# Last stage of a hybrid DeltaNet / HGRN2 block: gates stored in row order, the final norm on three engines, stores from GpSimd's queue, a third bank for the branch products

## The chip, the cores and the metric

One core of a Trainium2 chip. The metric is the device time of one execution in microseconds (us). All arithmetic is float32; products on TensorE split each float32 into a high and a low part of type fp32r and sum three passes (high x high, low x high, high x low).

## The reference, cut to what matters

A block over 2048 latent tokens (a grid of 32 rows and 64 columns, in row order) with a prefix of 256 context tokens. Two token mixers (A: gated DeltaNet, in row order; B: HGRN2, in column order) give `o_a` and `o_b`; then

```
def merge_branches(o_a, o_b, p, ...):
    y_a = rms_norm_gated(o_a, a_norm_l, p['a_gate']) @ w_a_out_l      # o * rsqrt(mean o^2) * gain * silu(gate)
    y_b = rms_norm_gated(o_b, b_norm_l, p['b_gate']) @ w_b_out_l
    gates = sigmoid(p['merge'])                                       # 2 x 1024 per token
    return (gates[0] * y_a + gates[1] * y_b) @ w_out_l
...
h_lat = layer_norm(alpha * h_lat + gate_l * sub_lat) * ln_g + ln_b
```

`a_gate`, `b_gate` and `merge` are columns of one input projection `u @ w_in`: 8 blocks of 128 columns for the branch gates, 16 for the merge gates.

## The kernel before, in words

The stages up to about 1862 us are the normalised and modulated input, the input projection (24 matmuls of 512 columns for each block of 128 outputs and 512 tokens), the convolution, and the two scans. Latent tokens are kept there in column order. `gate_block` (L212) makes one gate block: it projects, evicts the PSUM tile into `gt` (ScalarE on odd token groups L218, VectorE on even L220) and stores it in DRAM as `gT`; 24 blocks x 4 groups = 96 evictions, spread over the whole program.

The last stage (L1136 on) goes over 8 tiles of 256 tokens (4 grid columns x 32 rows, twice), `tg` = 0..7. For each tile:

- `pre(tg)`: loads the two mixers' outputs (`o`), takes 16 sums of squares on ScalarE (L1046), a power on GpSimd (L1050), scales (L1052). For four pairs of heads it loads the gate (`gt`), forms the gated SiLU (L1063, L1064), transposes `o` on TensorE into PSUM `ptw` (L1069), multiplies (L1071), and splits into `yh` (ScalarE, L1072) and `yl` (GpSimd, L1073). `o` is in row order within 128 tokens and the gate in column order, so L1071 reads PSUM through `by_row`.
- `branch_y(tg)`: for `m` = 0..7 (blocks of 128 of the 1024 channels) loads the two merge gates (`mg`, three buffers, L1082), takes their sigmoid (ScalarE, L1083), makes 24 matmuls of 256 columns into one PSUM bank `py` (L1089 to L1091; two banks, pool `pj2`, in turn), multiplies by the gates (VectorE, L1092), adds the branches (L1093), and splits into `mh` (ScalarE, L1095) and `ml` (VectorE, L1096). The last two write with `by_row`, 16 bytes apart, to turn column order into row order.
- `emit(tg)`: for two halves `t` of 128 tokens loads `x` into `xt` (two buffers), makes 2 x 24 matmuls of 512 columns (`pso`, L1109 to L1111), adds (L1112), takes the statistics (L1117 to L1119 and the power on GpSimd, L1120), normalises: VectorE (x - mean) * rs (L1130), GpSimd times `lng` (L1131), GpSimd plus `lnb` (L1132), and SyncE's queue stores it (L1133). The last tile has its own tail (L1121 to L1128), which the change doesn't touch.

All loads and stores stand in one queue, SyncE's (SP), in program order; a waiting entry holds what is behind it. A scheduler sets each engine's order of instructions from its own model of time, so the tiles overlap: `pre(tg + 1)` runs within tile `tg`, and the first three `mg` loads of a tile are made during the tile before. PSUM in the last stage: `py` 2 banks, `ptw` 3, `pso` 3.

Of the kernel before, what the change touches and what calls it, by code (L numbers as in the profile page):

```python
# [8 lines left out]
F32 = mybir.dt.float32  # L9
F32R = mybir.dt.float32r  # L10
U8 = mybir.dt.uint8
AF = mybir.ActivationFunctionType
ALU = mybir.AluOpType
# [3 lines left out]
P = 128  # L17
# [6 lines left out]
GR = SEQ // GW  # L24
# [15 lines left out]
def block_kernel(ctx, tc, x, c, ctx_in, c_ctx, w_mod, b_mod, w_in, conv_w, a_log, dt_bias,  # L40
                 lb_param, a_norm_g, b_norm_g, w_a_out, w_b_out, w_out, ln_g, ln_b, out, dbg=None):
    nc = tc.nc
    sy, te, ve, ac, po = nc.sync, nc.tensor, nc.vector, nc.scalar, nc.gpsimd
# [17 lines left out]
    MLV = 1  # L61
# [100 lines left out]
    def by_row(ap):  # L162
        return ap.rearrange("p (t r c) -> p t c r", r=GR, c=4)

    def by_col(ap):
        return ap.rearrange("p (t c r) -> p t c r", r=GR, c=4)

# [44 lines left out]
    def gate_block(i, groups, psum=None, tag="pj", w=None):  # L212
        w = w or load_w(gcol[i])
        for g in groups:
            ps = proj(w, g, psum or pg_[0], tag)
            t = re.tile([P, GT], F32, tag="acc", name="gt", bufs=2)
            if g % 2:
                ac.copy(out=t, in_=ps)  # L218
            else:
                ve.tensor_copy(out=t, in_=ps)  # L220
            sy.dma_start(out=gT[i, :, g * GT:g * GT + GT], in_=t)


# [788 lines left out]
    with tc.tile_pool(name="ww", reuse_waits="tile", bufs=2) as ww, \  # L1012
# [22 lines left out]
        def pre(tg):  # L1035
# [21 lines left out]
            for k in range(0, 8, 2):  # L1057
                i, h = divmod(k, H)
                gt = (wpp.tile([P, 2, TG], F32, tag="ws", name="gt", bufs=1) if tg == 0 and k == 6 else
                      ww.tile([P, 2, TG], F32, tag="g", name="gt", bufs=GBF))  # L1060
                sy.dma_start(out=gt, in_=gT[k:k + 2, :, tg * TG:tg * TG + TG].rearrange("h p t -> p h t"))
                sg = ww.tile([P, 2, TG], F32, tag="sg", name="sgt", bufs=SGB)
                ac.activation(out=sg, in_=gt, func=AF.Sigmoid)  # L1063
                ve.scalar_tensor_tensor(out=gt, in0=gt, scalar=cols[:, R_GA + i:R_GA + i + 1], in1=sg,  # L1064
                                        op0=ALU.mult, op1=ALU.mult)
                pt = pw_.tile([P, 2, TG], F32, tag="t", name="ptw", bufs=3)
                for j in range(2):
                    for t in range(2):
                        te.transpose(pt[:, j, t * P:t * P + P], on[t][:, i, h + j, :], ident)  # L1069
                gf = by_col(gt.rearrange("p j t -> p (j t)"))  # L1070
                last[0] = ve.tensor_tensor(out=gf, in0=by_row(pt.rearrange("p j t -> p (j t)")), in1=gf, op=ALU.mult).ins  # L1071
                ac.copy(out=yh[i][:, h:h + 2, :], in_=gt)  # L1072
                po.tensor_tensor(out=yl[i][:, h:h + 2, :], in0=gt, in1=yh[i][:, h:h + 2, :].bitcast(F32), op=ALU.subtract)  # L1073
            return yh, yl

        def branch_y(tg, yh, yl):
            mh = ww.tile([P, KB, TG], F32R, tag="mh", name="mh", bufs=1)
            ml = ww.tile([P, KB, TG], F32R, tag="ml", name="ml", bufs=1)
            for m in range(KB):
                mg = (wpp.tile([P, 2, TG], F32, tag="ws", name="mg", bufs=1) if MG3 and m % 3 == 2 else  # L1080
                      re.tile([P, 2, TG], F32, tag="acc", name="mg", bufs=2))
                sy.dma_start(out=mg, in_=gT[8 + m:24:8, :, tg * TG:tg * TG + TG].rearrange("i p t -> p i t"))  # L1082
                ac.activation(out=mg, in_=mg, func=AF.Sigmoid)  # L1083
                py = pj[0].tile([P, 2, TG], F32, tag="pj", name="py")
                ms_ = slice(m * P, m * P + P)
                for i in range(2):
                    wh, wl = wab[i]
                    for k in range(H):
                        te.matmul(out=py[:, i, :], lhsT=wh[:, k, ms_], rhs=yh[i][:, k, :], start=(k == 0), stop=False)  # L1089
                        te.matmul(out=py[:, i, :], lhsT=wh[:, k, ms_], rhs=yl[i][:, k, :], start=False, stop=False)  # L1090
                        te.matmul(out=py[:, i, :], lhsT=wl[:, k, ms_], rhs=yh[i][:, k, :], start=False, stop=(k == H - 1))  # L1091
                ve.tensor_tensor(out=mg, in0=py, in1=mg, op=ALU.mult)  # L1092
                ve.tensor_tensor(out=mg[:, 0], in0=mg[:, 0], in1=mg[:, 1], op=ALU.add)  # L1093
                mm, hm, lm = by_col(mg[:, 0]), by_row(mh[:, m, :]), by_row(ml[:, m, :])
                ac.copy(out=hm, in_=mm)  # L1095
                (ve if MLV else po).tensor_tensor(out=lm, in0=mm, in1=hm.bitcast(F32), op=ALU.subtract)  # L1096
            return mh, ml

        def emit(tg, mh, ml):
            for t in range(2):  # L1100
# [26 lines left out]
                                                op0=ALU.mult, op1=ALU.add)  # L1127
                        sy.dma_start(out=out_cm[:, 4 * cc:4 * cc + 4, ns], in_=xt[:, ns])  # L1128
                else:
                    ve.tensor_scalar(out=xt, in0=xt, scalar1=mv[:, 0:1], scalar2=rs_, op0=ALU.subtract, op1=ALU.mult)  # L1130
                    po.tensor_tensor(out=xt, in0=xt, in1=lng, op=ALU.mult)  # L1131
                    po.tensor_tensor(out=xt, in0=xt, in1=lnb, op=ALU.add)  # L1132
                    sy.dma_start(out=out_cm[:, 4 * cc:4 * cc + 4], in_=xt)  # L1133


        while late[0] < NLATE:  # L1136
# [52 lines left out]
```

## Time and profile before

| | us |
|---|---|
| median of 3 runs (lowest, highest) | 2328.68 (2319.0, 2331.19) |
| the profiled execution | 2322.79 |
| its span in the trace | 2321.1 |
| TensorE busy, share of the span | 2210.0, 95% |
| VectorE, ScalarE, GpSimd busy | 1401.9, 907.8, 756.9 |
| last matmul of the program starts | 2312.21 |

The profiled execution is 1.7 us longer than its span. TensorE is busy nearly throughout. A matmul's listed duration overlaps the next one's, so the time that it takes is read from the distance of two starts.

### The profile page before, as it was taken

What the parts mean: (1) busy time and instruction counts of PE and PEld (TensorE: products, weight loads), DVE (VectorE), ACT (ScalarE), POOL (GpSimd) and SP (SyncE); (2) the same over time, 40 slices, a digit from 0 to 9 for tenths busy, and PEclk for the clock granted to TensorE, in tenths of its full rate; (3) what the DMA queues carried; (4) which work ended last, traced back from release to release, by engine and by line L of the source; (5) the groups of instructions that cost most, each with busy time, mean ns of one, the idle gap of its engine ahead of it and who ended that gap; (6) DMA issues with size and microseconds to landing.
All of it is one profiled execution on the core that took longest, in us unless ns stands there. A gap on an engine that the chain in (4) does not pass through costs nothing. (4 is left out here: it accounts for less than half of the span.)

```text
span 2321.1 us, 39923 instructions
## 1 busy us (share of the span) xinstructions
PE 2210.0 (95%) x14998; PEld 1848.3 (80%) x14998; DVE 1401.9 (60%) x3184; ACT 907.8 (39%) x2298; POOL 756.9 (33%) x736
## 2 busy tenths in 40 slices
PE   7899999999999999999989999999989889999998
PEld 2778888888888888888878778788878878878887
DVE  5926666636766667774374877872332358566655
ACT  3523222234343444432434445544544454344321
POOL 3613343302221122224534445311133234334341
PEclk8999999999999999999999999999999999999999
DMA  8312222322322322224656588786887855434322
GB/s 317 112 36 73 66 73 71 87 63 78 92 71 85 91 74 87 85 76 132 178 163 195 185 243 256 206 240 204 250 271 264 264 192 166 127 110 128 118 82 78
DMA packets 298329, 330.24 MB, mean 142 GB/s; under 512 B 77536, under 2 KB 216918, under 8 KB 298136
## 3 DMA queue, kind: packets, MB, share of 16 engines
q1 hardware_dynamic: 298135, 327.69, 45.9%
q8 instruction: 118, 1.93, 0.4%
q14 instruction: 76, 0.61, 0.1%
HBM read 216.83 MB, written 110.79 MB: 141 GB/s over the span
## 5 line engine op out<-in xcount | busy, mean ns | idle before, releaser
L205 PE MATMUL ps<-uhi,wh 128*128 128x512 f32 (+1 forms) x1824 | 707.9, 388 | 5.4 <-DVE uhi L293 2.6
L206 PE MATMUL ps<-ulo,wh 128*128 128x512 f32 (+1 forms) x1824 | 705.8, 387 | 3.0 <-DVE ulo L295 2.7
L207 PE MATMUL ps<-uhi,wl 128*128 128x512 f32 (+1 forms) x1824 | 706.2, 387 | 0.5 <-POOL wl L197 0.5
L205 PEld LDWEIGHTS ps<-uhi,wh 128*128 128x128 f32 x1824 | 345.6, 190 | 71.0 <-DVE uhi L293 3.9
L206 PEld LDWEIGHTS ps<-ulo,wh 128*128 128x128 f32 x1824 | 345.7, 190 | 66.8 <-DVE ulo L295 3.9
L207 PEld LDWEIGHTS ps<-uhi,wl 128*128 128x128 f32 x1824 | 345.2, 189 | 64.5 <-POOL wl L197 1.3
L197 POOL TENSOR_TENSOR wl<-ws,wh 128x512 fp32r<-128x512 f32 x144 | 192.2, 1335 | 536.7 <-ACT wh L196 512.3
L196 ACT CAST wh<-ws 128x512 fp32r<-128x512 f32 x144 | 89.5, 621 | 288.5 <-DMA ws<-in_w_in_dram 192.3
L1089 PE MATMUL py<-yh,wab 128*128 128x256 f32 x512 | 151.4, 296 | 26.5 <-DVE mg L1092 25.6
L393 DVE SCALAR_TENSOR_TENSOR acc<-raw,cols,acc 128x512 f32<-128x512 f32 x192 | 153.9, 855 | 0.8
L1090 PE MATMUL py<-yl,wab 128*128 128x256 f32 x512 | 148.3, 290 | 2.6 <-POOL yl L1073 2.6
L1091 PE MATMUL py<-yh,wab 128*128 128x256 f32 x512 | 147.9, 289 | 0.0
L1089 PEld LDWEIGHTS py<-yh,wab 128*128 128x128 f32 x512 | 100.7, 197 | 31.0 <-DVE mg L1092 29.0
L572 POOL TENSOR_TENSOR bg<-s,fz 128x512 f32<-128x512 f32 (+1 forms) x36 | 38.0, 1057 | 263.5 <-ACT X L552 96.9
L1109 PE MATMUL pso<-uhi,mh 128*128 128x512 f32 x256 | 102.9, 404 | 3.6 <-ACT mh L1095 2.3
L1090 PEld LDWEIGHTS py<-yl,wab 128*128 128x128 f32 x512 | 101.0, 197 | 3.8 <-POOL yl L1073 3.2
L1111 PE MATMUL pso<-uhi,ml 128*128 128x512 f32 x256 | 102.0, 404 | 2.0 <-DVE ml L1096 1.9
L1110 PE MATMUL pso<-ulo,mh 128*128 128x512 f32 x256 | 101.6, 399 | 0.0
L1091 PEld LDWEIGHTS py<-yh,wab 128*128 128x128 f32 x512 | 101.2, 198 | 0.0
L1073 POOL TENSOR_TENSOR yl<-gt,yh 128x512 fp32r<-128x512 f32 x32 | 46.7, 1478 | 165.2 <-ACT yh L1072 165.2
L1096 DVE TENSOR_TENSOR ml<-mg,mh 128x256 fp32r<-128x256 f32 x64 | 53.0, 832 | 70.1 <-ACT mh L1095 69.4
L1095 ACT CAST mh<-mg 128x256 fp32r<-128x256 f32 x64 | 41.2, 651 | 135.7 <-DVE mg L1093 135.4
(371 smaller groups left out, 4135.8 us busy)
## 6 DMA issues: line engine op xcount, KB each, us to landing
ws<-in_w_in_dram SPq DMA_DIRECT2D x144, 256.0 KB, 3.2
gT<-gt SPq DMA_DIRECT2D x96, 256.0 KB, 3.2
kv<-knvD SPq DMA_DIRECT2D x36, 512.0 KB, 5.4
kq<-qkvD SPq DMA_DIRECT2D x32, 512.0 KB, 5.5
an<-atN SPq DMA_DIRECT2D x32, 512.0 KB, 5.7
mg<-gT SPq DMA_DIRECT2D x64, 256.0 KB, 3.6
qkvD<-acc SPq DMA_DIRECT2D x48, 256.0 KB, 2.3
l<-qkvD SPq DMA_DIRECT2D x16, 768.0 KB, 5.1
```

The costliest lines, as they stand in the source:

```text
L196: ac.copy(out=wh[:, j:j + 4, :], in_=ws)
L197: po.tensor_tensor(out=wl[:, j:j + 4, :], in0=ws, in1=wh[:, j:j + 4, :].bitcast(F32), op=ALU.subtract)
L205: te.matmul(out=ps, lhsT=wh[:, k, :], rhs=uhi[gi][:, k, :], start=(k == 0), stop=False)
L206: te.matmul(out=ps, lhsT=wh[:, k, :], rhs=ulo[gi][:, k, :], start=False, stop=False)
L207: te.matmul(out=ps, lhsT=wl[:, k, :], rhs=uhi[gi][:, k, :], start=False, stop=(k == KB - 1))
L393: ve.scalar_tensor_tensor(out=a_, in0=raw[:, o + k:o + k + n], scalar=wk, in1=a_, op0=ALU.mult, op1=ALU.add)
L1089: te.matmul(out=py[:, i, :], lhsT=wh[:, k, ms_], rhs=yh[i][:, k, :], start=(k == 0), stop=False)
L1090: te.matmul(out=py[:, i, :], lhsT=wh[:, k, ms_], rhs=yl[i][:, k, :], start=False, stop=False)
L1091: te.matmul(out=py[:, i, :], lhsT=wl[:, k, ms_], rhs=yh[i][:, k, :], start=False, stop=(k == H - 1))
L1109: te.matmul(out=ps, lhsT=mh[:, k, ts_], rhs=wout[0][k][:, ns], start=(k == 0), stop=False)
L1110: te.matmul(out=ps, lhsT=mh[:, k, ts_], rhs=wout[1][k][:, ns], start=False, stop=False)
L1111: te.matmul(out=ps, lhsT=ml[:, k, ts_], rhs=wout[0][k][:, ns], start=False, stop=(k == KB - 1))
```

## The change

It touches four things.

1. `gate_block` turns the order at eviction: the output is written through `as_rows` (contiguous) and the PSUM tile is read through `col_to_row` (steps of 32 elements), so `gT` holds row order. L1071, `mh` and `ml` then need no rearrangement and read and write contiguously.
2. `py` of m = 2 and 5 goes to a bank of its own (tag `y` of pool `pw`); `ptw` has 2 banks instead of 3.
3. The final norm of tiles 0 to 6: a small VectorE operation forms -mean * rs (`nm`), ScalarE applies scale and bias, VectorE multiplies by `lng`, GpSimd adds `lnb`.
4. The store of tiles 0 to 6 is issued by GpSimd (`po.dma_start`) instead of SyncE.

```diff
+    def col_to_row(ap):
+        return ap.rearrange("p (t c r) -> p t r c", r=GR, c=4)
+    def as_rows(ap):
+        return ap.rearrange("p (t r c) -> p t r c", r=GR, c=4)
...
             if g % 2:
-                ac.copy(out=t, in_=ps)
+                ac.copy(out=as_rows(t), in_=col_to_row(ps))
             else:
-                ve.tensor_copy(out=t, in_=ps)
+                ve.tensor_copy(out=as_rows(t), in_=col_to_row(ps))
...
-                pt = pw_.tile([P, 2, TG], F32, tag="t", name="ptw", bufs=3)
+                pt = pw_.tile([P, 2, TG], F32, tag="t", name="ptw", bufs=2)
...
-                gf = by_col(gt.rearrange("p j t -> p (j t)"))
-                last[0] = ve.tensor_tensor(out=gf, in0=by_row(pt.rearrange("p j t -> p (j t)")), in1=gf, op=ALU.mult).ins
+                last[0] = ve.tensor_tensor(out=gt, in0=pt, in1=gt, op=ALU.mult).ins
...
-                py = pj[0].tile([P, 2, TG], F32, tag="pj", name="py")
+                py = (pw_.tile([P, 2, TG], F32, tag="y", name="py", bufs=1) if m % 3 == 2 else
+                      pj[0].tile([P, 2, TG], F32, tag="pj", name="py"))
...
-                mm, hm, lm = by_col(mg[:, 0]), by_row(mh[:, m, :]), by_row(ml[:, m, :])
-                ac.copy(out=hm, in_=mm)
-                (ve if MLV else po).tensor_tensor(out=lm, in0=mm, in1=hm.bitcast(F32), op=ALU.subtract)
+                ac.copy(out=mh[:, m, :], in_=mg[:, 0])
+                (ve if MLV else po).tensor_tensor(out=ml[:, m, :], in0=mg[:, 0], in1=mh[:, m, :].bitcast(F32), op=ALU.subtract)
...
-                    ve.tensor_scalar(out=xt, in0=xt, scalar1=mv[:, 0:1], scalar2=rs_, op0=ALU.subtract, op1=ALU.mult)
-                    po.tensor_tensor(out=xt, in0=xt, in1=lng, op=ALU.mult)
+                    nm_ = ww.tile([P, 1], F32, tag="nm", name="nm2")
+                    ve.scalar_tensor_tensor(out=nm_, in0=mv[:, 0:1], scalar=-1.0, in1=rs_, op0=ALU.mult, op1=ALU.mult)
+                    ac.activation(out=xt, in_=xt, func=AF.Identity, scale=rs_, bias=nm_)
+                    ve.tensor_tensor(out=xt, in0=xt, in1=lng, op=ALU.mult)
                     po.tensor_tensor(out=xt, in0=xt, in1=lnb, op=ALU.add)
-                    sy.dma_start(out=out_cm[:, 4 * cc:4 * cc + 4], in_=xt)
+                    po.dma_start(out=out_cm[:, 4 * cc:4 * cc + 4], in_=xt)
```

Up to the last stage the order on GpSimd, SyncE, ScalarE and VectorE is the same as before. In it the scheduler places several things otherwise. (Lines below are those of each kernel; the changed one is 5 to 7 lines further down.)

VectorE at the border of two tiles, before: from the statistics of the second half to the second branch product.

```order
L1118 BN_AGGR mv_21251<-st_21250 128x2
L1119 TENSOR_SCALAR rs_21252<-mv_21251 128x1
L1130 TENSOR_SCALAR xt<-xt,mv_21251,rs_21252 128x1024
L1092 TENSOR_TENSOR mg<-py,mg 128x512
L1093 TENSOR_TENSOR mg<-mg 128x256
L1096 TENSOR_TENSOR ml<-mg,mh 128x2x4x32
L1092 TENSOR_TENSOR mg<-py,mg 128x512
```

The same place now:

```order
L1123 BN_AGGR mv_21273<-st_21272 128x2
L1124 TENSOR_SCALAR rs_21274<-mv_21273 128x1
L1136 SCALAR_TENSOR_TENSOR nm_21280<-mv_21273,rs_21274 128x1
L1098 TENSOR_TENSOR mg<-py,mg 128x512
L1099 TENSOR_TENSOR mg<-mg 128x256
L1138 TENSOR_TENSOR xt<-xt,lng 128x1024
L1101 TENSOR_TENSOR ml<-mg,mh 128x256
L1098 TENSOR_TENSOR mg<-py,mg 128x512
```

`nm` still stands ahead of the first product of the tile and needs the power on GpSimd; the multiplication by `lng` comes after it, between the add and `ml`. GpSimd in the same place, before:

```order
L1120 TENSOR_TENSOR rs_20706<-rs_20706,nhalf 128x1
L1131 TENSOR_TENSOR xt<-xt,lng 128x1024
L1132 TENSOR_TENSOR xt<-xt,lnb 128x1024
L1120 TENSOR_TENSOR rs_20772<-rs_20772,nhalf 128x1
L1131 TENSOR_TENSOR xt<-xt,lng 128x1024
L1132 TENSOR_TENSOR xt<-xt,lnb 128x1024
```

and now:

```order
L1125 TENSOR_TENSOR rs_21206<-rs_21206,nhalf 128x1
L1056 TENSOR_TENSOR ms<-ms,nhalf 128x8
L1139 TENSOR_TENSOR xt<-xt,lnb 128x1024
L1140 DMA out_dram<-xt 32x4x1024
L1125 TENSOR_TENSOR rs_21274<-rs_21274,nhalf 128x1
L1139 TENSOR_TENSOR xt<-xt,lnb 128x1024
L1140 DMA out_dram<-xt 32x4x1024
```

The power of the second half now stands behind one addition and the first half's store, instead of behind a multiplication and an addition. ScalarE at the end of a tile's branch products, now:

```order
L1088 ACTIVATE mg<-mg 128x512
L1100 CAST mh<-mg 128x256
L1088 ACTIVATE mg<-mg 128x512
L1077 CAST yh_21094<-gt 128x512
L1088 ACTIVATE mg<-mg 128x512
L1100 CAST mh<-mg 128x256
L1077 CAST yh_21094<-gt 128x512
```

The last `mh` of a tile (the second L1100 here, m = 7) stands behind two sigmoids of the next tile's merge gates. On SyncE a tile's `xt` loads now stand ahead of the `mg` loads of m = 3 and m = 6, with no store between them. On TensorE the transposes, which were strewn over the branch products, now come in two lots of 8 within the output product.

## Rows read from the trace of the kernel before

**Rows 1.** Busy time by stretch: start:end, length, busy time of each engine (instructions), granted TensorE clock, DMA share, GB/s. The whole steady part of the last stage, two of its tiles, and a stretch of 3.3 us just behind a gap.
```profile
1897.00:2313.00 416.00, 386.31 (x2368) 342.05 (x2368) 267.23 (x410) 151.19 (x403) 151.65 (x88) 0.97 0.37 118
2004.36:2058.72 54.36, 49.07 (x286) 43.15 (x287) 32.88 (x54) 19.73 (x56) 20.22 (x12) 0.94 0.37 117
2217.22:2268.10 50.88, 46.57 (x286) 41.72 (x284) 27.72 (x44) 12.56 (x21) 16.39 (x10) 0.97 0.33 108
2126.90:2130.20 3.30, 3.30 (x18) 3.30 (x17) 1.84 (x4) 0.84 (x2) 0.00 (x0) 0.50 0.66 225
```

**Rows 2.** TensorE's matmuls by line from 1897 to 2313 us: shapes, count | busy us, mean ns | idle us just before them, and what ended it. (L1091 and L1110 have the counts of L1089 and L1109 and no idle time.)
```profile
L1089 PE MATMUL py<-yh,wab 128*128 128x256 f32 x496 | 146.3, 295 | 25.6 <-DVE mg L1092 25.6
L1090 PE MATMUL py<-yl,wab 128*128 128x256 f32 x496 | 143.0, 288 | 1.5 <-POOL yl L1073 1.5
L1109 PE MATMUL pso<-uhi,mh 128*128 128x512 f32 x256 | 102.9, 404 | 3.6 <-ACT mh L1095 2.3 <-DVE xt L1112 1.2
L1111 PE MATMUL pso<-uhi,ml 128*128 128x512 f32 x256 | 102.0, 404 | 2.0 <-DVE ml L1096 1.9
```

**Rows 3.** TensorE in order of time around the border of tiles 3 and 4: start us, duration, instruction [idle before, what ended it].
```profile
2100.00 0.39 PE L1109 MATMUL pso<-uhi,mh 128*128 128x512 f32 x1
...
2105.60 0.39 PE L1109 MATMUL pso<-uhi,mh 128*128 128x512 f32 x1
...
2106.30 0.28 PE L1089 MATMUL py<-yh,wab 128*128 128x256 f32 x1
...
2109.14 0.28 PE L1089 MATMUL py<-yh,wab 128*128 128x256 f32 x1
...
2111.99 1.14 PE L1069 MATMUL ptw<-ident,o 128*128 128x128 f32 x9
...
2118.15 0.38 PE L1089 MATMUL py<-yh,wab 128*128 128x256 f32 x1 [2.17 <-DVE mg L1092]
...
2126.21 0.38 PE L1089 MATMUL py<-yh,wab 128*128 128x256 f32 x1 [1.77 <-DVE mg L1092]
```

**Rows 4.** VectorE over the same border, in order of time.
```profile
2111.23 0.81 DVE L1130 TENSOR_SCALAR xt<-xt,mv,rs 128x1024 f32<-128x1024 f32 x1 [2.42 <-POOL rs L1120]
2111.96 0.68 DVE L1092 TENSOR_TENSOR mg<-py,mg 128x512 f32<-128x512 f32 x1
2112.68 2.11 DVE L1093 TENSOR_TENSOR mg<-mg 128x256 f32<-128x256 f32 x1
2115.57 1.92 DVE L1096 TENSOR_TENSOR ml<-mg,mh 128x256 fp32r<-128x256 f32 x1 [0.78 <-ACT mh L1095]
2117.41 0.68 DVE L1092 TENSOR_TENSOR mg<-py,mg 128x512 f32<-128x512 f32 x1
...
2124.94 0.62 DVE L1096 TENSOR_TENSOR ml<-mg,mh 128x256 fp32r<-128x256 f32 x1 [3.50 <-ACT mh L1095]
```

**Rows 5.** GpSimd over the same border, in order of time.
```profile
2105.82 2.41 POOL L1131 TENSOR_TENSOR xt<-xt,lng 128x1024 f32<-128x1024 f32 x1 [0.93 <-DVE xt L1130]
2108.30 2.38 POOL L1132 TENSOR_TENSOR xt<-xt,lnb 128x1024 f32<-128x1024 f32 x1
2110.64 0.55 POOL L1120 TENSOR_TENSOR rs<-rs,nhalf 128x1 f32<-128x1 f32 x1
...
2114.58 2.44 POOL L1132 TENSOR_TENSOR xt<-xt,lnb 128x1024 f32<-128x1024 f32 x1
```

**Rows 6.** SyncE's queue from 1900 to 2300 us, the longest waits that concern stores and `xt` loads (us in total, times, longest); then DMA rows: the merge-gate loads (KB each, median us from issue to landing), and the stores of L1133 (ns of one issue min/median/max, first and last start; us to landing min/median/max).
```profile
SPq L1133 <- POOL rs L1120: 52.3, 5, 10.7
SPq L1103 <- DMA out_dram<-xt: 36.1, 14, 3.7
...
mg<-gT SPq DMA_DIRECT2D x64, 256.0 KB, 3.6
...
L1133 SPq DMA_DIRECT2D out_dram<-xt x14: 595/597/1459, 1955.9 to 2276.6; - x14
DMA to landing us min/median/max: 3.0/4.0/4.3
```

**Rows 7.** Durations of single operations over the whole program: count, ns min/median/max, first and last start us, shapes.
```profile
L1093 DVE TENSOR_TENSOR mg<-mg x64: 402/426/2647, 1898.9 to 2295.4; 128x256 f32<-128x256 f32 x64
L1095 ACT CAST mh<-mg x64: 622/656/701, 1900.8 to 2295.9; 128x256 fp32r<-128x256 f32 x64
L1096 DVE TENSOR_TENSOR ml<-mg,mh x64: 605/636/2011, 1902.5 to 2296.6; 128x256 fp32r<-128x256 f32 x64
L1083 ACT ACTIVATE mg<-mg x64: 612/632/635, 1888.1 to 2290.6; 128x512 f32<-128x512 f32 x64
L1026 ACT CAST uhi<-ws x8: 1027/1035/1051, 1890.7 to 1930.5; 128x1024 fp32r<-128x1024 f32 x8
L273 ACT ACTIVATE xn<-xn,nm,rs x5: 1239/1243/1245, 23.6 to 89.3; 128x1024 f32<-128x1024 f32 x5
L1027 DVE TENSOR_TENSOR ulo<-ws,uhi x4: 1209/1214/1224, 1895.8 to 1932.9; 128x1024 fp32r<-128x1024 f32 x4
L381 ACT COPY raw<-ps x48: 567/588/602, 151.1 to 430.1; 128x512 f32<-128x512 f32 x48
L218 ACT COPY gt<-ps x48: 566/580/670, 80.7 to 1882.2; 128x512 f32<-128x512 f32 x48
L1071 DVE TENSOR_TENSOR gt<-ptw,gt x32: 669/681/692, 1882.2 to 2251.2; 128x512 f32<-128x512 f32 x32
```

## The prediction

> **What bounds the kernel now.** I read the page's first two parts first: TensorE is busy 95% of the span. So only its gaps and its slow stretches can be won, and the change touches the last stage alone, apart from the gate evictions. Then busy time by stretch [rows 1]: the part with all eight tiles, 1897 to 2313 us, takes 416 us; a tile takes 54.4 us early and 50.9 late. Then TensorE in order of time [rows 3], for what it needs: 24 matmuls of 512 columns start within 2105.60 - 2100.00 = 5.60 us, 24 of 256 columns within 2109.14 - 2106.30 = 2.84 us, 9 transposes take 1.14 us, 0.127 each. By the counts [rows 2] the stretch holds 3 x 496 / 24 = 62 branch units (176.1 us), 3 x 256 / 24 = 32 output units (179.2 us), and 7 tiles x 16 transposes (14 us): 369 us. So **47 us of the 416 are excess**. TensorE's waits account for 25.6 + 1.5 + 3.6 + 2.0 = 32.7 us of it [rows 2], and 25.6 of these are a branch unit that waits for VectorE to empty its PSUM bank. The other 14 us are clock: 416 us at a mean of 0.97 is 12.5 us lost [rows 1]. The slow stretches come behind waits: after the 1.77 us wait that ends at 2126.21 the granted clock is 0.50 from 2126.90 to 2130.20, the lower level of 1.2 GHz [rows 1, 3]. Per us waited I therefore count 14 / 32.7 = 0.43 us of clock on top: 1.43 us in all.
>
> **Why VectorE is late.** Let P = 2106.30 be the start of a tile's first branch unit. It ends at P+2.8, but its product with the gates starts at 2111.96 = P+5.7 [rows 4]: ahead of it stands L1130, 2.42 us idle for the power of the second half, which on GpSimd stands behind L1131 and L1132 of the first half [rows 5]. Then L1093 takes 2.11 us and L1096 1.92, where their medians are 0.43 and 0.64 [rows 4, 7]: GpSimd is in L1131 and L1132 just then. So the second product starts at P+11.1, and the third branch unit, which needs the first bank again, and the fourth are held up. That is the 2.17 us wait. The second wait (1.77 us) goes back to the merge gates: L1096 idles 3.50 us for `mh` [rows 4], because ScalarE has a sigmoid ahead of it that waits for its load, and the load could start only when the late `ml` freed its buffer. SyncE's queue adds to it: stores wait there for GpSimd (52.3 us) and `xt` loads for the stores to land (36.1 us), with `mg` loads behind both [rows 6].
>
> **The change, part by part.**
>
> *Row order.* `mh` and `ml` become contiguous. `ml` then is like L1093, 0.43 instead of 0.64 us. `mh` on 256 elements: from 632 ns for 512 and 1035 for 1024 the slope gives 0.43 instead of 0.66 [rows 7]. That is 0.44 us off the chain of each m. The price is 96 evictions that read PSUM with a step of 128 bytes. ScalarE has a row for that, L381: 588 ns against 580 for L218. VectorE has none at this step; L1071 reads at 16 bytes and takes 681, as much as the contiguous L1092's 0.68. From below 0; from above what 16-byte steps cost a write, 0.21 us per 256, so 0.42 per eviction. I take 0. Either is hidden: the next tile's 24 matmuls of 5.6 us run meanwhile in another bank.
>
> *Third bank.* TensorE now first needs the first product's bank for m = 3, not m = 2: 2.84 us of slack. The two `ptw` banks cost nothing, as transposes now come in lots of 8 with the output product around them.
>
> *Norm.* ScalarE gains 2 x 1.24 us per tile (L273 does the same operation [rows 7]) and loses 8 x 0.23; VectorE's L1130 (0.81) turns into 1.21 (as L1027) plus a small one. GpSimd loses L1131, 2.4 us, twice a tile, and the collision with it. The addition remains, so one of the two collisions at P remains.
>
> *Stores.* SyncE no longer stops for GpSimd; the `xt` loads still wait there for the store to land, 4.0 us [rows 6]. The GpSimd price X of issuing one store has no row. Nearest below: SyncE's issue of the same store, 0.60 us. Above: a whole GpSimd pass over as many elements, 2.4 us. I take X = 1.0, nearer the issue, since that is the same transfer.
>
> The Trainium skill (SBUF — State Buffer, section "SBUF: two separate sides") says that a transfer issued by GpSimd has its descriptors written by that engine, which is locked out while VectorE runs an operation in a two-port mode: its example goes from 620 to 3100 ns. With 3.1 us for X my sum would be 2319 instead of 2298; no run of the kernel before has such a transfer.
>
> **The new timetable of a tile**, from the orders shown above. ScalarE's normalisation of the first half stands behind all 16 squares of the next tile, so `lng` for it ends near P+1, its addition on GpSimd near P+3.4, its store at P+4.4, the second power at P+5.0. The first product is at **P+5.3**, hardly earlier than P+5.7. Then 0.68 + 0.43 for it and the add, 1.21 for `lng`, 0.43 for `ml`: the second product starts near **P+8.1, not P+11.1**. TensorE needs the two banks at P+8.5 and P+11.4 and doesn't wait. Round of a merge-gate buffer: load 3.6, sigmoid 0.63, product 0.68, add 0.43, `mh` 0.43, `ml` 0.43 and some 0.4 of hand-overs, 6.6 us, against three branch units, 8.5 us. So the second wait goes too, though VectorE stays about 2 us behind at the end.
>
> **What is late next** is the last `mh`. It now stands behind a sigmoid of the next tile, whose load can start only after `ml` of m = 6. With VectorE 2 us behind at the end of the branch units (Q), that `ml` is done at Q+1.1, load 3.7, sigmoid 0.6, one `yh` 0.6, a second sigmoid 0.6, then `mh` 0.4: Q+7. TensorE wants it after 8 transposes and 21 output matmuls, Q+5.9. Wait: 1.1 us; with the stray waits of a few tenths that `ml` shows now I take 1.6 per tile.
>
> **Sum.** Waits left: 7 x 1.6 + 4 for the first tile, whose output-weight preparation stays = 15.2 instead of 32.7; saved 17.5 us, with the clock's share 17.5 x 1.43 = 25 us. The last tile's tail behind the last matmul is unchanged. The profiled execution took 2322.79 us, so **2298 us**. That execution stands 5.9 us below the median of the three runs, within their 12 us; I add nothing for it. About 0.5%, 11.6 us, is what a measurement of this kernel tells from no change: faster means under 2317, slower over 2340.
>
> **Bounds.** Best: all waits but the first tile's 4 go, (32.7 - 4) x 1.43 = 41 us: 2282. Each us of X shifts the first product and so the whole chain of the tile: 7 x 1.43 = 10 us. X = 2.4 gives 2312, X = 0.6 gives 2294. Merge-gate loads at 4.4 instead of 3.6 us add 0.8 per tile, 8 us: 2306. Both together: 2320.
>
> **Rivals.**
>
> 1. *All waits close* (0.16). For it: the third bank and 1.9 us to spare in the gates' round. Against: the order on ScalarE. 2282 us.
> 2. *The wait moves to GpSimd's queue* (0.15). The store's issue meets VectorE operations that hold GpSimd up, as GpSimd held up L1093 by 1.7 us [rows 4, 7]; X = 1.0 + 1.7 = 2.7 and more, 2315 to 2322 us: about no change. Against: L1130 is gone, and of VectorE's work near the store only the products with two operands in SBUF were seen to collide. The Trainium skill's page quoted above describes such a lock; the prices here are from rows alone.
> 3. *Slower: the store stops GpSimd's queue* (0.06). The place is between the first half's addition and the second half's power, on which `nm`, and behind it the first product, wait. At 10 us per us of X the gain is gone at X = 3.5 (2323) to 4.1 (the old median); the run is over 2340 from X = 5.2, twice GpSimd's longest regular operation of this size; at X = 6 it is 2348. Against: no row of this stage shows an issue above 1.46 us.
>
> That the change does not do what it says can be left out: the orders show `mh` and `ml` as 128x256, and the stores on GpSimd.
>
> **Chances.** Forecast 0.63 (2286 to 2312), rivals 0.16, 0.15, 0.06. Faster: forecast, rival 1 and a third of rival 2, 0.84; same: 0.10; slower: 0.06. The range leaves out rival 3 and the upper part of rival 2 and takes in the bounds: 2280 to 2320.
>
> **What would show it.** Right: TensorE's idle time for the gate products falls from 25.6 us to under 6, that for the last `mh` and `ml` rises from 4.2 to about 11; tiles of 48 to 50 us; `mh` and `ml` medians near 0.43; gate evictions unchanged; the second product about 2.8 us after the first. Wrong: a GpSimd store that lasts over 2.5 us ahead of the second power, a first product later than P+7, `xt` loads that hold the m = 6 gates beyond P+20, or evictions with a 128-byte step above 0.8 us.

## The result, and the profile after

The changed kernel takes **2302.95 us** (median of 4 runs, 2295.09 to 2305.59) against 2328.66 (median of 4) for the kernel before: ratio 0.9891, 95% interval 0.9867 to 0.9915. The forecast was 2298, range 2280 to 2320. The profiled execution took 2301.48 us with a span of 2299.7, 21.4 less than the 2321.1 of before.

I cut the span at the start of VectorE's last gate eviction. What follows, "the stage" from here on, takes 2321.1 - 1881.6 = 439.5 us before and 2299.7 - 1886.8 = 412.9 now: **26.6 us less**. What comes ahead ended 5.2 us later in this execution. Over all profiles below that point lies between 1881.6 and 1895.4, whichever order the gates have, so this says nothing of the change, and I compare stages. A stage is read from one execution of its kernel, so a difference of a few us between two stages is weaker than one of medians with an interval.

Busy time by stretch (columns as in [rows 1]). The kernel before, its whole stage up to the last tile's tail:

```profile
1884.60:2312.60 428.00, 393.82 (x2414) 348.94 (x2414) 271.74 (x413) 157.29 (x418) 159.13 (x93) 0.97 0.38 122
```

After: the same stretch, its part from the second tile's fourth branch unit on, and two tiles, cut at their first gate product.

```profile
1889.80:2291.20 401.40, 382.64 (x2417) 340.81 (x2416) 260.25 (x428) 161.95 (x432) 136.14 (x93) 0.99 0.41 130
1961.80:2291.20 329.40, 321.93 (x2039) 286.52 (x2038) 205.18 (x352) 124.11 (x326) 105.10 (x76) 1.00 0.39 121
2011.03:2059.38 48.35, 46.72 (x298) 41.58 (x297) 31.55 (x56) 20.73 (x58) 17.11 (x12) 1.00 0.42 131
2107.49:2157.06 49.57, 48.56 (x314) 43.43 (x312) 31.38 (x56) 20.97 (x58) 16.24 (x12) 1.00 0.41 128
```

401.4 us instead of 428.0; tiles of 48 to 50 us where [rows 1] had 54.4 and 50.9; and from 1961.8 us on the granted clock is 1.00, 2.4 GHz. All of the gain lies behind the first two tiles: from the first branch unit of the first tile to that of the third it takes 112.6 us before (1883.6 to 1996.2) and 112.8 now (1889.7 to 2002.5). TensorE's matmuls by line in the whole stretch (columns as in [rows 2]):

```profile
L1095 PE MATMUL py<-yh,wab 128*128 128x256 f32 x512 | 146.1, 287 | 8.5 <-DVE mg L1098 7.6 <-ACT yh L1077 0.9
L1114 PE MATMUL pso<-uhi,mh 128*128 128x512 f32 x256 | 102.8, 403 | 7.2 <-ACT mh L1100 3.2 <-ACT uhi L1032 2.4 <-DVE xt L1117 1.6
L1116 PE MATMUL pso<-uhi,ml 128*128 128x512 f32 x255 | 101.4, 398 | 0.6 <-DVE ml L1101 0.6
L1075 PE MATMUL ptw<-ident,o 128*128 128x128 f32 x113 | 15.6, 276 | 2.4 <-DVE gt L1076 2.4
```

The wait for a gate product fell from 25.6 [rows 2] to 7.6 us. The same view from 1961.8 us on shows how little of it recurs:

```profile
L1095 PE MATMUL py<-yh,wab 128*128 128x256 f32 x424 | 120.3, 284 | 2.9 <-DVE mg L1098 2.9
L1114 PE MATMUL pso<-uhi,mh 128*128 128x512 f32 x224 | 89.6, 400 | 3.3 <-ACT mh L1100 3.2
L1116 PE MATMUL pso<-uhi,ml 128*128 128x512 f32 x223 | 88.1, 395 | 0.6 <-DVE ml L1101 0.6
L1075 PE MATMUL ptw<-ident,o 128*128 128x128 f32 x96 | 12.7, 274 | 0.7 <-DVE gt L1076 0.7
```

Now the border of two tiles. TensorE: the first branch unit starts at P = 2099.91, the fourth (m = 3, which needs the first bank again) at 2108.45 without a wait.

```profile
2099.91 0.28 PE L1095 MATMUL py<-yh,wab 128*128 128x256 f32 x1
...
2108.45 0.28 PE L1095 MATMUL py<-yh,wab 128*128 128x256 f32 x1
```

VectorE there, the counterpart of [rows 4]:

```profile
2100.18 1.23 DVE L1138 TENSOR_TENSOR xt<-xt,lng 128x1024 f32<-128x1024 f32 x1 [0.70 <-ACT xt L1137]
2101.32 0.69 DVE L1122 BATCH_NORM_STATS2 st<-xt 128x6 f32<-128x512 f32 x1
2101.93 3.04 DVE L1058 TENSOR_TENSOR o<-o,ms 128x1024 f32<-128x1024 f32 x1
...
2107.42 0.16 DVE L1136 SCALAR_TENSOR_TENSOR nm<-mv,rs 128x1 f32<-128x1 f32 x1 [0.70 <-POOL rs L1125]
2107.49 0.68 DVE L1098 TENSOR_TENSOR mg<-py,mg 128x512 f32<-128x512 f32 x1
...
2110.37 0.68 DVE L1098 TENSOR_TENSOR mg<-py,mg 128x512 f32<-128x512 f32 x1
2111.09 1.91 DVE L1099 TENSOR_TENSOR mg<-mg 128x256 f32<-128x256 f32 x1
2113.47 0.43 DVE L1101 TENSOR_TENSOR ml<-mg,mh 128x256 fp32r<-128x256 f32 x1 [0.47 <-ACT mh L1100]
...
2119.11 0.42 DVE L1101 TENSOR_TENSOR ml<-mg,mh 128x256 fp32r<-128x256 f32 x1 [2.20 <-ACT mh L1100]
...
2124.03 0.42 DVE L1101 TENSOR_TENSOR ml<-mg,mh 128x256 fp32r<-128x256 f32 x1 [1.47 <-ACT mh L1100]
```

GpSimd there, as in [rows 5]:

```profile
2101.49 2.40 POOL L1139 TENSOR_TENSOR xt<-xt,lnb 128x1024 f32<-128x1024 f32 x1 [1.20 <-DVE xt L1138]
2104.18 0.60 POOL L1140 DMA_DIRECT2D out_dram<-xt  x1 [0.30 <-POOL xt L1139]
2106.81 0.57 POOL L1125 TENSOR_TENSOR rs<-rs,nhalf 128x1 f32<-128x1 f32 x1 [2.03 <-DVE rs L1124]
2110.19 2.51 POOL L1139 TENSOR_TENSOR xt<-xt,lnb 128x1024 f32<-128x1024 f32 x1 [2.81 <-DVE xt L1138]
```

The first product starts at 2107.49 = P+7.6, later than before (P+5.7), and its bank is free at P+8.3. With three banks it is wanted at P+8.5, which leaves 0.2 us. The second product follows at P+10.5. Both additions on GpSimd collide with an operation of VectorE that reads two operands from SBUF: o's scale lasts 3.04 us, the add of the branches 1.91.

The operations, as in [rows 7], then SyncE's longest wait for a store, as in [rows 6]:

```profile
L1100 ACT CAST mh<-mg x64: 387/392/408, 1907.6 to 2270.5; 128x256 fp32r<-128x256 f32 x64
L1101 DVE TENSOR_TENSOR ml<-mg,mh x64: 409/425/2643, 1909.3 to 2271.0; 128x256 fp32r<-128x256 f32 x64
L1058 DVE TENSOR_TENSOR o<-o,ms x16: 1165/1227/3044, 1880.2 to 2199.9; 128x1024 f32<-128x1024 f32 x16
L224 ACT COPY gt<-ps x48: 567/580/670, 80.7 to 1887.3; 128x512 f32<-128x512 f32 x48
L226 DVE COPY gt<-ps x48: 675/691/693, 73.0 to 1886.8; 128x512 f32<-128x512 f32 x48
L1140 POOL DMA_DIRECT2D out_dram<-xt x14: 584/598/778, 1964.8 to 2254.7; - x14
DMA to landing us min/median/max: 3.0/3.2/5.7
```
```profile
SPq L1108 <- DMA out_dram<-xt: 98.9, 10, 17.4
```

`mh` and `ml` take 0.39 and 0.43 us, gate evictions are unchanged, a store's issue takes GpSimd 0.60 us. SyncE's wait for the stores to land grew from 36.1 to 98.9 us without harm: at this border the `xt` load at 2117.14 still starts 2.4 us ahead of the free `mg` buffer (2119.53, behind `ml`) that the queue needs next, and at every border the gate load of m = 6 starts 0.03 us behind the `ml` that frees its buffer.

### The profile page after: what moved, and what is told of

Same layout as the page of the kernel before. It is cut to its first block, busy times and chain, and to the rows that moved or that the text cites. A ratio compares the mean times of both kernels' runs of the same rounds, so it can differ in the third digit from the quotient of the medians.

```text
span 2299.7 us, 39916 instructions
## 1 busy us (share of the span) xinstructions
PE 2201.6 (96%) x14998; PEld 1843.8 (80%) x14998; DVE 1391.9 (61%) x3198; ACT 912.9 (40%) x2312; POOL 734.8 (32%) x736
## 5 line engine op out<-in xcount | busy, mean ns | idle before, releaser
L1095 PE MATMUL py<-yh,wab 128*128 128x256 f32 x512 | 146.1, 287 | 8.5 <-DVE mg L1098 7.6
L1097 PE MATMUL py<-yh,wab 128*128 128x256 f32 x512 | 144.4, 282 | 0.0
L1095 PEld LDWEIGHTS py<-yh,wab 128*128 128x128 f32 x512 | 97.5, 191 | 10.9 <-DVE mg L1098 9.2
L1097 PEld LDWEIGHTS py<-yh,wab 128*128 128x128 f32 x512 | 97.6, 191 | 0.2
L402 POOL TENSOR_TENSOR acc<-acc,sg 128x512 f32<-128x512 f32 (+1 forms) x56 | 71.5, 1295 | 46.3 <-ACT sg L401 46.3
L1088 ACT ACTIVATE mg<-mg 128x512 f32<-128x512 f32 x64 | 40.4, 632 | 112.0 <-DMA mg<-gT 112.0
```

## The experiments

Theory A: the third bank carries the gain, because it gives TensorE 2.85 us of patience. Theory B: the relief of GpSimd (norm and store) carries it, because it brings VectorE's first product forward. The first eight kernels undo each part in the changed kernel (u_...) or make it alone in the kernel before (o_...). The edits are the hunks of the change above:

- **bank**: `py` with the tag `y` for `m % 3 == 2`, and `ptw` with 2 buffers
- **rows**: `col_to_row`/`as_rows` at the gates' eviction; L1071, `mh`, `ml` without rearrangement
- **norm**: the four lines with `nm_`, ScalarE and VectorE in place of `ve.tensor_scalar` and GpSimd's `lng`
- **store**: `po.dma_start` in place of `sy.dma_start`

All results (stage as defined above, of the one profiled execution of each kernel; waits of TensorE in it for a gate product and for `mh`; start of the first and second product at a border in the middle, from P):

| kernel | median us | ratio to before, 95% | stage us | waits: product, `mh` | products at P+ |
|---|---|---|---|---|---|
| before | 2328.66 | | 439.5 | 25.6, 2.3 | 5.7, 11.1 |
| changed | 2302.95 | 0.9891 [0.9867, 0.9915] | 412.9 | 7.6, 3.2 | 7.6, 10.5 |
| u_bank | 2318.23 | 0.9966 [0.9948, 0.9984] | 430.8 | 17.8, 0.4 | 5.6, 8.5 |
| u_rows | 2320.33 | 0.9969 [0.9955, 0.9983] | 429.2 | 10.8, 10.2 | 8.5, 11.6 |
| u_norm | 2318.07 | 0.9961 [0.9944, 0.9978] | 427.9 | 19.5, 4.2 | 8.9, 14.1 |
| u_store | 2314.13 | 0.9941 [0.9919, 0.9963] | 418.9 | 8.1, 7.6 | 7.7, 10.5 |
| o_bank | 2331.1 | 1.0017 [1.0002, 1.0032] | 442.8 | 15.6, 9.4 | 7.9, 13.3 |
| o_rows | 2319.59 | 0.9964 [0.9950, 0.9978] | 427.1 | 20.1, 1.6 | 5.6, 10.8 |
| o_norm | 2321.17 | 0.9981 [0.9969, 0.9993] | 434.7 | 17.6, 5.4 | 5.5, 8.5 |
| o_store | 2336.52 | 1.0046 [1.0031, 1.0061] | 448.6 | 31.2, 1.0 | 6.9, 12.3 |
| x_delay | 2312.54 | 0.9935 [0.9915, 0.9955] | 425.9 | 14.7, 5.9 | 5.4, 9.5 |
| v_dve | 2296.9 | 0.9875 [0.9853, 0.9897] | 407.7 | 6.6, 2.4 | 6.9, 9.0 |
| v_add | 2304.29 | 0.9897 [0.9878, 0.9916] | 416.5 | 7.1, 6.1 | 7.1, 10.0 |
| v_dve2 | 2301.64 | 0.9886 [0.9866, 0.9905] | 413.2 | 12.3, 2.0 | 6.7, 8.8 |

The medians of before that the ratios stand against are 2325.66 to 2328.66.

### One part undone

**u_bank.** `py` back in two banks, `ptw` in three.

> The changed kernel with the branch products back in two PSUM banks in turn and ptw in three; all else as changed. Theory A (the third bank carries the gain, by giving TensorE 2.8 us of slack per tile and by moving the transposes out of the branch products): the wait of branch units for VectorE comes back to 15 to 25 us, tiles of 51 to 53 us, time 2317 to 2326. Theory B (GpSimd's shorter work and the contiguous mh and ml carry it): waits under 12 us, time 2303 to 2311.

Stage +17.9 us. Its first two products are two us *earlier* than in the changed kernel, and yet TensorE waits 17.8 us for products. VectorE around the wait in one of its tiles (P = 2050.4), then ScalarE, then TensorE:

```profile
2061.78 0.42 DVE L1100 TENSOR_TENSOR ml<-mg,mh 128x256 fp32r<-128x256 f32 x1 [0.47 <-ACT mh L1099]
...
2067.46 0.42 DVE L1100 TENSOR_TENSOR ml<-mg,mh 128x256 fp32r<-128x256 f32 x1 [3.72 <-ACT mh L1099]
...
2069.42 0.42 DVE L1100 TENSOR_TENSOR ml<-mg,mh 128x256 fp32r<-128x256 f32 x1 [0.48 <-ACT mh L1099]
```
```profile
2066.50 0.63 ACT L1088 ACTIVATE mg<-mg 128x512 f32<-128x512 f32 x1 [3.61 <-DMA mg<-gT]
2067.04 0.39 ACT L1099 CAST mh<-mg 128x256 fp32r<-128x256 f32 x1
```
```profile
2068.54 0.48 PE L1094 MATMUL py<-yh,wab 128*128 128x256 f32 x1 [2.25 <-DVE mg L1097]
```

This is the second wait of the kernel before, still there: an `ml` frees a merge-gate buffer, its load takes some 3.5 us (the median in the changed kernel), ScalarE's queue has the sigmoid of that load ahead of an `mh` that is ready, and `ml` and the product behind it stand still. Here the sigmoid of m = 4 stands ahead of the `mh` of m = 2. The `ml` of m = 1, 2 and 3 start at 2061.78, 2067.46 and 2069.42, so two branch units take 7.64 us, and TensorE needs 2 x 2.85 = 5.70 for them: the round is slower than TensorE. The changed kernel has a round too, but another order on ScalarE, the sigmoid of m = 4 ahead of the `mh` of m = 3:

```profile
2118.15 0.63 ACT L1088 ACTIVATE mg<-mg 128x512 f32<-128x512 f32 x1 [2.76 <-DMA mg<-gT]
2118.69 0.39 ACT L1100 CAST mh<-mg 128x256 fp32r<-128x256 f32 x1
```

Two units take 5.64 us there (`ml` of m = 1 at 2113.47, of m = 3 at 2119.11), then 4.92 (2124.03): it keeps pace. So the edit takes back two things at once, the patience of the third bank and the order that the scheduler made with it, and this run doesn't tell them apart. Time and product wait are as theory A has them (2317 to 2326 us, 15 to 25 us).

**u_rows.** Gates stored in column order again, the rearrangements back in L1071, `mh` and `ml`.

> The changed kernel with gates stored in column order and mh, ml written 16 bytes apart as before. Their medians are 0.65 and 0.64 us again. Theory A: 0.44 us per m adds 3.5 us to VectorE's and ScalarE's work of a tile, mostly behind TensorE: 2304 to 2310. Theory B: it is on the chain of each m, waits for mh and ml of m = 7 double, 2311 to 2318. If the strided evictions of the gates cost anything before the last stage, the last gate eviction starts earlier than 1886.8 us by over 3 us.

Stage +16.3 us. `mh` is 0.64 us again and the late part of the tile slips: the wait for the last `mh` is 10.2 us instead of 3.2, that for products 10.8. The median, 2320.33, lies above both theories: the 0.44 us of each m cost more than either had.

**u_norm.** VectorE's `tensor_scalar` and GpSimd's two passes again, the store still GpSimd's.

> The changed kernel with the old final norm (VectorE subtract and scale, GpSimd times lng, GpSimd plus lnb), store still issued by GpSimd. Theory A: the third bank absorbs most of the lateness, 2305 to 2311. Theory B: the two GpSimd passes again hold up the add and ml of the first product (1.7 and 1.3 us) and the second power, tiles of 50 to 52 us, 2312 to 2322.

Stage +15.0 us. GpSimd and VectorE at the border (P = 2107.0):

```profile
2107.82 2.40 POOL L1136 TENSOR_TENSOR xt<-xt,lng 128x1024 f32<-128x1024 f32 x1
2110.29 3.27 POOL L1137 TENSOR_TENSOR xt<-xt,lnb 128x1024 f32<-128x1024 f32 x1
```
```profile
2107.88 3.42 DVE L1058 TENSOR_TENSOR o<-o,ms 128x1024 f32<-128x1024 f32 x1 [0.21 <-POOL ms L1056]
```

The first half's two passes lengthen the scale ahead of the first product (P+8.9); the second half's collide with the add and `ml` behind it (2.10 and 1.98 us), so the second product stands at P+14.1, where even with three banks its bank is wanted free by P+11.4. That is over what the third bank covers, as theory B had it.

**u_store.** The store issued by SyncE again.

> The changed kernel with the stores issued by SyncE's queue again. Theory A: SyncE waits for GpSimd's addition ahead of the merge-gate loads of m = 3 and m = 6, up to 1 us per tile: 2303 to 2309. Theory B (stores in SyncE's queue were a main cause of late gates): 2311 to 2318.

Stage +6.0 us. The products stand where they stood. SyncE's queue waits for GpSimd's addition, then for the store to land, and only then has the second `xt` load and the gate load of m = 6 behind it. That gate load starts 0.41 to 0.99 us behind the `ml` that frees its buffer in the six tiles from the third on, and the wait for the last `mh` rises to 7.6 us:

```profile
SPq L1140 <- POOL xt L1139: 75.3, 7, 14.4
```

The median is 11.2 us longer, in theory B's range; 6.0 us of stage would be in A's. The runs don't decide between the two.

### One part alone

**o_bank**, **o_rows**, **o_norm**, **o_store**: each hunk of the list above put into the kernel before.

> The kernel before with the third bank for the branch products alone (ptw 2 banks), norm, stores and row order as before. Theory A: TensorE's wait for the products falls from 25.6 us to under 12, time 2305 to 2315. Theory B: only about 5 us are won, 2320 to 2326.

> The kernel before with the gates in row order alone. Theory A: mh and ml drop to 0.40 and 0.43 us, but the first product and the collisions with GpSimd stay: 2320 to 2327. Theory B: 0.44 us off each m's chain is felt in full, 2308 to 2318.

> The kernel before with the final norm spread over three engines alone, stores by SyncE. Theory A: one collision of two goes, 1.5 to 2 us per tile: 2313 to 2322. Theory B: the main cause, 2303 to 2312.

> The kernel before with the stores issued by GpSimd alone. Each issue occupies GpSimd 0.6 us (as in the changed kernel), ahead of the second half's power, so the first product is 0.6 to 1 us later; SyncE no longer stops for GpSimd. Theory A: the two about cancel, 2322 to 2332. Theory B (SyncE's queue was a main cause): 2310 to 2320.

Stages: +3.3 us (bank), -12.4 (rows), -4.8 (norm), +9.1 (store). Their sum is -4.8, that of the four medians +2.6 us (against 2326.45, the median of before in these runs); together they give -26.6 of the stage. Of the theories only A of o_norm holds; o_rows lies between its two, o_bank and o_store above both of theirs. A alone and B alone both fall: the third bank by itself gains nothing, norm and store by themselves little or less than nothing, and each is worth 6 to 18 us where the others are in place. Norm and store as a pair were not put into the kernel before, but u_bank is rows, norm and store together, and its stage, 430.8 us, is no better than that of rows alone, 427.1. The bank alone turns product waits (25.6 to 15.6) into waits for `mh` (2.3 to 9.4), because its order puts the last `mh` behind a sigmoid of the next tile (in the tile from 2116.9 that sigmoid waits 1.27 us for its load and TensorE 1.62 for `mh`). The store alone is the one part that costs, and its place is the one that rival 3 named. GpSimd and VectorE of o_store:

```profile
2122.91 2.39 POOL L1132 TENSOR_TENSOR xt<-xt,lnb 128x1024 f32<-128x1024 f32 x1
2125.59 0.63 POOL L1133 DMA_DIRECT2D out_dram<-xt  x1 [0.30 <-POOL xt L1132]
2126.25 0.58 POOL L1120 TENSOR_TENSOR rs<-rs,nhalf 128x1 f32<-128x1 f32 x1
```
```profile
2126.86 0.81 DVE L1130 TENSOR_SCALAR xt<-xt,mv,rs 128x1024 f32<-128x1024 f32 x1 [3.43 <-POOL rs L1120]
```

The power waits behind the store, and VectorE idles 3.43 us instead of 2.42 [rows 4]. 0.92 us of store for 9.1 us of stage is the 10 us per us of the prediction, though not its make-up: product waits rise by 5.6 us (25.6 to 31.2), 0.8 a tile, and the clock (0.96 over 437.1 us, against 0.97 over 428.0) adds more than the 0.43 us per us waited that the prediction counted.

### The delay made longer, and the work moved to VectorE

**x_delay.** Behind each GpSimd store stands another power of 1.65 us:

```diff
                     po.dma_start(out=out_cm[:, 4 * cc:4 * cc + 4], in_=xt)
+                    dl = ww.tile([P, 8], F32, tag="dl", name="dl", bufs=1)
+                    po.tensor_tensor(out=dl, in0=mv[:, 0:1].to_broadcast([P, 8]), in1=nhalf.to_broadcast([P, 8]), op=ALU.pow)
```

> The changed kernel with one more power of 128x8 on GpSimd (1.65 us, result unused) behind each store, so that the second half's power, nm and the first product of a tile come about 1.6 us later. The third bank is free at P+8.3 and wanted at P+8.5 in the changed kernel, so there is no slack left there. Theory P (the prediction's price, every us on GpSimd between the halves costs 1.0 to 1.4 us per tile): 7 x 1.6 x 1.0 to 1.4 = 11 to 16 us, 2312 to 2317. Theory S (the gates' loads and ScalarE's order set the tile, and the first product has slack): under 4 us, 2300 to 2305.

Stage +13.0 us, 8 us per us, and a median in theory P's range. But it isn't the pure shift that was meant, so it is no test of P's reason: the scheduler answered by putting `nm` behind the first product. VectorE at its border:

```profile
2112.65 0.68 DVE L1098 TENSOR_TENSOR mg<-py,mg 128x512 f32<-128x512 f32 x1
...
2116.38 0.16 DVE L1136 SCALAR_TENSOR_TENSOR nm<-mv,rs 128x1 f32<-128x1 f32 x1 [2.59 <-POOL rs L1125]
2116.45 0.42 DVE L1101 TENSOR_TENSOR ml<-mg,mh 128x256 fp32r<-128x256 f32 x1
```

The first product is early (P+5.4), but the first `ml` stands behind `nm`, so the gates' round starts late: TensorE's long wait of the tile (2.00 us) comes at P+19. A delay on GpSimd costs through whichever of the two waits is behind it.

**v_dve.** The norm as two passes of VectorE, none on ScalarE or GpSimd; the store stays on GpSimd:

```diff
-                    nm_ = ww.tile([P, 1], F32, tag="nm", name="nm2")
-                    ve.scalar_tensor_tensor(out=nm_, in0=mv[:, 0:1], scalar=-1.0, in1=rs_, op0=ALU.mult, op1=ALU.mult)
-                    ac.activation(out=xt, in_=xt, func=AF.Identity, scale=rs_, bias=nm_)
-                    ve.tensor_tensor(out=xt, in0=xt, in1=lng, op=ALU.mult)
-                    po.tensor_tensor(out=xt, in0=xt, in1=lnb, op=ALU.add)
+                    ve.scalar_tensor_tensor(out=xt, in0=xt, scalar=mv[:, 0:1], in1=lng, op0=ALU.subtract, op1=ALU.mult)
+                    ve.scalar_tensor_tensor(out=xt, in0=xt, scalar=rs_, in1=lnb, op0=ALU.mult, op1=ALU.add)
```

> The changed kernel with the norm of tiles 0 to 6 in two VectorE passes, (x - mean) * lng and * rs + lnb, as the last tile has it; no ScalarE and no GpSimd pass, store still by GpSimd. Theory P (a late first product is what is left of a tile's excess, and it is late because GpSimd's addition meets VectorE's scale of o): no collisions, first product at P+3.5 to P+5 instead of P+7.6, tiles of 47 to 47.8 us, 2292 to 2298. Theory S: 2299 to 2304. A third case, VectorE becomes the bound with 2.9 us of norm per half: 2305 or more.

**v_add.** The changed kernel's norm with `ve.tensor_tensor` in place of `po.tensor_tensor` for the addition of `lnb`.

> The changed kernel with the addition of lnb on VectorE (1.2 us) instead of GpSimd. The two collisions (1.8 us on the scale of o, 1.5 us on the second add) go, and 1.2 us of VectorE work comes in the same two places: first product P+7.0 to P+7.4, second about P+10. Theory P: 0 to 0.6 us per tile, 2297 to 2302. If the collisions cost more than their length: under 2296.

v_dve has the shortest time and stage of all (2296.9 and 407.7 us). In total time it isn't told from the changed kernel (the intervals overlap); its stage is 5.2 us shorter. VectorE's long operations are no longer held up: its two passes take 1.28 us each, o's scale 1.23. GpSimd's powers are, by these passes: that of the second half takes 1.47 us where the changed kernel has 0.57. The first product does not wait for it:

```profile
2108.20 1.47 POOL L1125 TENSOR_TENSOR rs<-rs,nhalf 128x1 f32<-128x1 f32 x1 [3.21 <-DVE rs L1124]
```

Two tiles of v_dve are

```profile
2062.20:2109.20 47.00, 47.00 (x307) 42.51 (x306) 30.09 (x56) 18.34 (x56) 13.98 (x11) 1.00 0.43 136
2158.60:2205.50 46.90, 46.44 (x296) 41.45 (x296) 29.90 (x56) 18.39 (x56) 13.86 (x11) 1.00 0.43 135
```

By [rows 3] a tile needs 8 x 2.84 + 4 x 5.60 + 16 x 0.127 = 47.2 us of TensorE: these tiles stand at that floor; the one between them takes 49.4. The median is in theory P's range, but P's reason isn't shown: the first product stands at P+6.9, not at P+3.5 to P+5. v_add speaks against it. There VectorE makes the addition, the hand-over to ScalarE and back remains, and the first two products come where they were expected (P+7.1, P+10.0), ahead of the changed kernel's; yet its time (2304.29, above both its theories) is level with that kernel. To take the addition alone away from GpSimd gains nothing. What v_dve's 5.2 us of stage come from stays open.

**v_dve2.** v_dve with two banks for `py` and three for `ptw`.

> The version whose norm is two passes of VectorE, with output product's banks back to two (and the transposes' to three). It asks whether the third bank is still needed where nothing collides. Two banks ask for the second product by the time the next tile's first pair of sums is due (the wait of TensorE on the products was 17.8 us in the changed kernel with two banks, against 7.6 with three). Theory 'the limits stand side by side, each binds where the others are gone': the first product stays at P+5 to P+7 whatever runs it, so two banks still make TensorE wait for it: product waits 14 to 20 us, stage 420 to 430 us (VectorE version with three banks: 407.7), about 2310 to 2316 us. Rival 'the third bank only absorbs the collisions of VectorE with GpSimd's addition': without the collisions the bank is worth little: product waits under 10 us, stage under 414 us, under 2302 us.

Stage 413.2 and 2301.64 us, as the rival had it, though its product wait, 12.3 us, is over the rival's 10 and under the theory's 14. The third bank is worth 5.5 us of stage here against 17.9 in the changed kernel (4.7 us of median, with overlapping intervals, against 15.3). That fits the rival, that most of its worth there was to absorb lateness from collisions and hand-overs with GpSimd and ScalarE, but doesn't show it: the first two products of u_bank (P+5.6, P+8.5) are no later than here (P+6.7, P+8.8), and ScalarE's order differs too. A part remains, the gates' round (a wait of 1.47 us at P+20 in one tile).

## Why the prediction was right, point by point

**What bounds the kernel: right.** The gain came from TensorE's waits and the clock behind them. By the view of [rows 2], taken over the whole stage, the listed waits were 34.6 us in the 428.0 us stretch (32.7 in the shorter one of the prediction), and are 8.5 + 7.2 + 0.6 + 2.4 = 18.7 in 401.4: 15.9 less. The clock lost 428.0 x 0.03 = 12.8 us and loses 401.4 x 0.01 = 4.0: 8.8 less, 0.55 us per us waited where the prediction counted 0.43 (the clock has two digits). Together 24.7 of the 26.6 us; 25 were forecast. The rate is no constant. The clock's loss comes in slow stretches such as the one in [rows 1], and over the same part of the program u_norm's 31.0 us of waits go with a granted clock of 0.98, o_norm's 28.9 us with 0.97. That 0.43 served here is in part luck.

**Row order: right.** `mh` 0.39, `ml` 0.43 (0.43 and 0.43 forecast); evictions with the 128-byte step 580 and 691 ns (580 and 688 contiguous).

**Price of the store, X: right in size, wrong in place.** 0.60 us of issue and 0.30 us ahead of it, 0.9 against the 1.0 taken. The step "each us of X shifts the first product and so the whole chain" holds for the old norm (o_store). In the changed kernel GpSimd idles 2.03 us ahead of the second power, which waits for VectorE, so the store lies beside that. The rule of the Trainium skill (SBUF — State Buffer, section "SBUF: two separate sides") from which the prediction took 3.1 us did not come into play: the page gives that time for a whole transfer beside a copy in a two-port mode, and no such copy ran beside a store here. The longest issue was 0.78 us, and the one at 2104.18 took 0.60 beside VectorE's two-operand scale of `o`.

**First product: wrong, P+7.6 for P+5.3.** The step that failed is "the second power at P+5.0". It ran from P+6.9 to P+7.5. The working left out o's scale, which stands between the first half's `lng` and the second half's statistics on VectorE, and put the collision with GpSimd's addition at the products alone. One addition meets the scale (3.04 for 1.22 us), the other the second add (1.91 for 0.42). This was listed as a sign of a wrong prediction, and the time held all the same, by luck: the bank is free at P+8.3 and wanted at P+8.5. The second product follows 2.9 us later, as forecast (2.8).

**The second wait: right in effect, wrong in cause.** The prediction found 1.9 us to spare in the gates' round because it took the round as one buffer's, 6.6 us for three units. In truth an `mh` stands behind a sigmoid that waits for a load, which ties successive buffers together: 5.64 and then 4.92 us for two units of 5.70, next to nothing to spare at first. In u_bank, with two banks and another order on ScalarE, two units take 7.64 us and the wait is back, 2.25 us in the tile shown. Which of the two differences removed it in the changed kernel isn't shown.

**Waits left: nearly right in sum, each term mis-sized.** 18.7 us for 15.2. Seven tiles keep 2.9 + 3.3 + 0.6 + 0.7 = 7.5 us, where 7 x 1.6 = 11.2 were counted (the last `mh` costs 0.5 a tile, not 1.1); the part up to 1961.8 us, the first tile and the border behind it, keeps 11.2, where 4 were counted. Part of that is the output-weight preparation (2.4 for `uhi`) and one wait of 4.75 us for a product at 1905.03. Two of the signs named for a right prediction failed with these terms: the waits for products are 7.6 us, not under 6, and those for the last `mh` and `ml` 3.2 + 0.6 = 3.8, not about 11. That the errors of the terms cancel in the sum is luck.

**How the parts work together: not foreseen.** The sum treated the four parts as terms. They are conditions: two banks (with the order that comes with them) make the gates' round bind, the old `mh` and `ml` or SyncE's stores make the last `mh` bind, the old norm makes the second product bind. Each undone brings its own wait back, so the four losses (55 us of stage) are twice the gain. Alone, row order gains 12.4 us of stage, and the four sum to 4.8. No rival spoke of the parts by themselves.

**Left open.** The first two tiles of v_dve, cut at their first gate product, still take 49.4 + 56.7 = 106.1 us where two floors are 94.4, and the change itself gained nothing in them. No run changed the weight preparation in them.

## What to carry to other kernels

Write for each buffer when it becomes free and when it is next wanted, counted from one mark of the loop, for all that ends in the same wait; a change pays where it moves the last of these, and parts of one change can be worth nothing alone and all of it together. A round through a load has to be followed through each engine's order, not only through its own buffer: what stands behind the operation that waits for the load belongs to the round. When a small operation is put on another engine, list everything on the receiving engine's way to it: here the missing 1.22 us operation, and what collides with it, put the first product 2.3 us off.

## What the runs showed of the hardware

- In the collisions shown here a VectorE operation with two operands in SBUF and a GpSimd pass over SBUF (128x1024) ran one after the other, but for some 0.15 us. In the changed kernel the addition ran from 2101.49 to 2103.89 and the scale of `o`, listed from 2101.93 to 2104.97, has 1.08 of its usual 1.23 us left after that. In u_norm they alternate: `lng` 2107.82 to 2110.22, the scale to 2111.30, and the second pass, begun at 2110.29, lasts 3.27 instead of 2.40 us, of which 2.26 lie behind the scale's end. Whichever starts first keeps the other waiting, as the Trainium skill says (SBUF — State Buffer, section "SBUF: two separate sides"), and these rows agree. VectorE's statistics and its add from PSUM, which ran in u_norm during that second pass, kept their 0.69 and 0.67 us.
- The one that waits need not be next. In the changed kernel a GpSimd pass (`ulo`) that starts at 1910.80, while a two-operand operation of VectorE runs, does not get its turn when that one ends: two more of VectorE's, each begun behind the one before without a gap, keep their usual 0.42 and 1.22 us, and the pass lasts 4.22 us, of which 2.30 lie behind the end of the last at 1912.72. And a `tensor_scalar` of 128x4 with a single operand, 0.16 us at other times, starts there at 1912.63 and lasts 2.41, to the end of that pass.
- The engine that issues a store does not set how long it flies: 512 KB landed in 3.2 us (median) when GpSimd issued it in the changed kernel, in 4.6 when GpSimd issued it in o_store, and in 4.0 by SyncE in u_store and before [rows 6].
- Reading PSUM with a step of 128 bytes cost an eviction nothing on ScalarE (580 ns for 580) or VectorE (691 for 688), while a 16-byte step on the side written cost `mh` 0.64 - 0.39 = 0.25 us per 256 elements (u_rows against the changed kernel).
